# W_down of a decoder trunk's MLP turned round: token blocks stand in the array, 512 weight columns move, and the sample's 32 tokens go unsplit through quarters of it

## Chip, cores and metric

One core of one Trainium2 chip runs the whole step as one program. Times are device microseconds (us) of that core. Three runs of the kernel before gave 2141.54, 2145.24 and 2144.73 us, median 2144.73. One more execution was profiled; its span, from the first instruction to the last, is 2147.1 us.

## The reference, cut to what matters

One layer of a decoder trunk for 256 prompt tokens and 32 sample tokens (8 x 4), all in float32, width D = 2048. The first part (input projection, four token-mixing branches, their merge, w_out) is the same in both kernels. What the change touches is the second sub-layer:

```
h = rmsnorm(x1, n_mlp_pre)                 # (tokens, 2048)
a = relu(h @ w_up) ** 2                    # w_up (2048, 8192)
f = a @ w_down                             # w_down (8192, 2048)
y = x1 + rmsnorm(f, n_mlp_post)            # y_prompt (256, 2048), y_sample (32, 2048)
```

## The kernel before

Activations lie transposed: 128 channels on the partitions, the 288 tokens (256 prompt, then 32 sample) in the columns. A dense product of the program is made exact enough by a split: an operand W is W = H + L, where H has the short mantissa of float32r and L is the rest, also float32r. Each product W x is then three float32r products, H xh, H xl and L xh, added up in PSUM.

**Weights.** `plan` lists the weight chunks (512 KB each, 1024 columns of a raw buffer) in the order of use and the jobs that use them. `w_load` issues a chunk's transfer on SyncE's queue into one of `RAWN` = 4 raw buffers. A chunk has two halves of 128 x 512. For a half, ScalarE writes H (`w_high`, a CAST) and VectorE writes L (`w_low`, a TENSOR_TENSOR subtract) into one of `HN` = 5 pairs of buffers. `w_split`, called after each tile of a half, lets these run up to four halves ahead of TensorE; `w_low` issues the next loads.

**Products.** `dense` goes over the halves of a group. A half of w_up or w_down is 2 tiles of K (128 rows each) by 256 weight columns. For each of the two output tiles of 128 channels, and each of the 2 tiles of K, three products are made: 128 x 128 weights stand, 288 token columns move. That is 12 products per half. PSUM banks rotate over five: `dps` (three), `holda`, `holdb`.

**The MLP.** The 8192 hidden channels come in four fourths (`nf = 4`): up (16 tiles of hidden channels, `ev_up`: relu, square, split into `tH`, `tL`), then down with those 16 tiles as K, over 16 output tiles. `ev_down` adds a fourth's product to `self.f` (channels on partitions, 288 tokens). In the last fourth it also adds up squares for the norm (`square`) and multiplies by the gain, and `lane_ftok` turns the result by 128 x 128 transposes so that tokens lie on the partitions. `finish` sums the squares by small products, makes the reciprocal root (`rsqrt`), adds x1 and stores y. The program is written out whole ahead of time; a planner (`Pace`) estimates when operands are there and interleaves the side work ("lanes") with the dense products. It counts no times on the chip; order on each engine is fixed by what it emits.

Every instruction goes through one helper, so nearly all have line L234; rows are told apart by tiles: `rfix` holds the split weights, `rt` holds `tH` and `tL`, `ffix` the raw weights and constants, `barena` the second half's float32 buffers, `rot` the banks of the lanes.

Of the kernel before, what the change touches and what calls it, by code (L numbers as in the profile page):

```python
# [10 lines left out]
ALU = mybir.AluOpType  # L11
# [25 lines left out]
class Tiles:  # L37
    """Columns lo..hi of each of some buffers, indexed as [:, tile, ...]."""
# [8 lines left out]
class Arena:  # L47
    """Blocks of columns. One given back is used again when its last use is estimated over, or if there is no other."""
# [66 lines left out]
class Step:  # L115
    """A chain of instructions: when its results will be there, when it goes on."""
# [5 lines left out]
class Pace:  # L122
    """An estimate of each engine's program in microseconds, so that work is emitted when its operands will be there."""
# [55 lines left out]
    def cost(self, eng, name, out, ins):  # L179
# [5 lines left out]
        if eng == "pe":  # L185
            if name == "transpose":
                return n * 2 / 2400
            return n * (1 if ins[-1].dtype == F32R else 4 if out.shape[0] > 32 else 1) / 2400
# [9 lines left out]
class Flags:  # L198
    """What is there, from when on."""
# [13 lines left out]
class Paced:  # L213
    """An engine whose instructions are counted."""
# [34 lines left out]
class Kern:  # L249
# [70 lines left out]
    def post(self, f):  # L320
        """f, which reads the last bank, behind the present unit."""
# [19 lines left out]
    def rsqrt_steps(self, y, v, t):  # L341
        """y = v ** -0.5 on the vector engine: a seed from the exponent's bits and Newton steps."""
# [91 lines left out]
    def gains(self):  # L434
        """Loads of the norms' gains as rows, the first one's before."""
# [9 lines left out]
    def vectors(self):  # L445
        """Loads of the other per-channel vectors and of the conv and pool states."""
# [29 lines left out]
    def lane_prep(self):  # L476
        """Columns of the vectors and of the states, by transposes."""
# [51 lines left out]
    def w_init(self, chunks):  # L529
# [8 lines left out]
        self.wh = [self.R.get(512).ap for _ in range(self.HN)]  # L538
        self.wl = [self.R.get(512).ap for _ in range(self.HN)]
        self.nload = 0  # L540
        self.nsplit = 0
        self.low, self.rawat = [], [0.0] * self.RAWN
        self.w_load()

    def w_load(self):
# [5 lines left out]
        raw = self.raw[i % self.RAWN]  # L551
        dst = raw[:, 0:nk * nc_].rearrange("p (k n) -> p k n", k=nk)
        if pad:
            self.nc.gpsimd.memset(raw[:, 0:nk * nc_], 0.0)
            at = 0
            for s in src:
                n = s.shape[-1]
                self.rawat[i % self.RAWN] = self.timed(lambda: self.nc.sync.dma_start(dst[:, :, at:at + n], s.rearrange("(k p) n -> p k n", p=128)))
                at += n
        else:  # L560
            self.rawat[i % self.RAWN] = self.timed(lambda: self.nc.sync.dma_start(dst, src.rearrange("(k p) n -> p k n", p=128)))

    def w_high(self):
        """Half a chunk of the split W = H + L: H, with float32r's mantissa."""
        i, k, n, nc_ = self.halves[self.nsplit]
        raw = self.raw[i % self.RAWN][:, k * nc_:(k + n) * nc_]
        h = self.wh[self.nsplit % self.HN][:, 0:n * nc_]
        l = self.wl[self.nsplit % self.HN][:, 0:n * nc_]
# [12 lines left out]
    def w_split(self, last):  # L581
        """Splits ahead, up to the half last, as far as their operands will be there."""
# [4 lines left out]
        if n <= last and n < len(self.halves) and self.rawat[self.halves[n][0] % self.RAWN] <= now + self.SOON[1]:  # L587
            self.w_high()

    def w_need(self, s):  # L590
        """The split of the half s."""
# [38 lines left out]
    def timed(self, f):  # L630
        """When the results of f will be there."""
# [27 lines left out]
    def room(self, *sizes):  # L659
        """Waits until blocks of these sizes can be had and some is left."""  # L660
# [35 lines left out]
    def bank(self):  # L696
        """The next bank for a tile's products, after the evacuation that reads it."""
# [12 lines left out]
    def dense(self, ci, nch, mts, x, evac, raw=0):  # L710
        """Groups of output tiles: chunks ci..ci+nch-1 over K, the tiles mts (tile, column offset)."""
# [8 lines left out]
        for s in hs:  # L720
            _, _, nk, ncol = self.halves[s]
            self.w_need(s)
            wh = self.wh[s % self.HN][:, 0:nk * ncol].rearrange("p (k n) -> p k n", k=nk)
            wl = self.wl[s % self.HN][:, 0:nk * ncol].rearrange("p (k n) -> p k n", k=nk)
            for m, off in mts:
# [12 lines left out]
                self.w_split(s + self.HN - 1)  # L738
# [6 lines left out]
    XRAW = 7  # L745

    def x_load(self, c):
        """Half the channels of x by tokens."""
# [22 lines left out]
    def x_init(self):  # L771
# [3 lines left out]
        # the first tiles' H, L, and their sums, which lie where k and v come later  # L775
# [1880 lines left out]
```

## Time and profile before

| what | value |
|---|---|
| runs, median (lowest to highest) | 2144.73 us (2141.54 to 2145.24) |
| profiled execution, span | 2147.1 us, 2.4 us above the median |
| TensorE busy | 2104.4 us, 98% of the span |
| VectorE / ScalarE busy | 60% / 45% |
| mean granted clock of TensorE | 0.985 of 2.4 GHz |
| four stretches of w_down products | 1411.3, 1616.1, 1820.8 and 2025.6 us to 2132.1 us |

How to read it: in the rows below, PE is TensorE's products and PEld its weight loads, DVE is VectorE, ACT is ScalarE. A product's own duration (about 0.3 us for 288 columns) is longer than its share of the engine, because products overlap; what one costs is read from start to start.

### The profile page before, as it was taken

Reading aid. Unit: us, or ns where it says so; the run is one execution under the profiler, and the core shown is the slowest. Engines: PE = TensorE matmul, PEld = TensorE weight load, DVE = VectorE, ACT = ScalarE, POOL = GpSimd, SP = SyncE. Lnnn points to the kernel's source line nnn. Section 1 sums busy time; section 2 is a strip of 40 time slices with the busy share of each in tenths; the row PEclk is TensorE's granted clock in tenths of the full one; section 3 lists DMA queues with packets and bytes.
Section 4 is the critical chain, followed back from the end, with each engine's and each line's share of the span. In section 5 each row is a group of like instructions: output and inputs, shape, how many; then the busy total and the mean of one; then the engine's idle time right before and its main releaser. Section 6 shows DMA issues by size and latency. Waiting matters only on the chain.

```text
span 2147.1 us, 43279 instructions
## 1 busy us (share of the span) xinstructions
PE 2104.4 (98%) x16452; PEld 2011.0 (94%) x16452; DVE 1280.3 (60%) x2534; ACT 968.6 (45%) x1864; POOL 74.4 (3%) x324
## 2 busy tenths in 40 slices
PE   7999999999999999999999999999999999999997
PEld 6999999999877788899999998999999999999997
DVE  4769997778754555465555547544555455445554
ACT  4445543335433333344444555644444344334454
POOL 4101100101000000000000000000000000000000
PEclk7999999999999999999999998999999999999998
DMA  5697777867788777656555653555555555555553
GB/s 157 190 244 203 187 189 198 223 170 211 216 232 267 227 231 216 197 149 168 165 164 169 202 158 109 155 168 162 163 164 170 164 163 165 167 166 162 164 158 113
DMA packets 359956, 388.98 MB, mean 181 GB/s; under 512 B 20729, under 2 KB 334259, under 8 KB 355652
## 3 DMA queue, kind: packets, MB, share of 16 engines
q1 hardware_dynamic: 359748, 386.22, 62.2%
q8 instruction: 129, 2.11, 0.4%
q14 instruction: 79, 0.65, 0.1%
HBM read 374.94 MB, written 11.23 MB: 180 GB/s over the span
## 4 chain that ended last, share of the span: by engine, by line
PE 92%; DMA 3%; DVE 2%; SPq 1%; issue 1%; ACT 0%; DVEq 0%; ACTq 0%
PE dps L234 66%; PE holda L234 11%; PE holdb L234 8%; PE rot L234 7%; DVE arena L234 1%; DMA arena<-cache_sb_k 1%; DMA arena<-state_ssm_h 1%; SPq L234 1%; DVE rfix L234 1%; DMA arena<-state_dn_conv 1%; DMA ffix<-w_in 1%; DVE barena L234 0%; DMA arena<-state_dn_s 0%; SPq L1265 0%; DMA arena<-x_prompt 0%
## 5 line engine op out<-in xcount | busy, mean ns | idle before, releaser
L234 PE MATMUL dps<-rfix 128*128 128x288 f32 x8124 | 1174.8, 299 | 6.7 <-DVE arena L234 2.7
L234 PEld LDWEIGHTS dps<-rfix 128*128 128x128 f32 x8124 | 1105.3, 189 | 47.4 <-issue 26.7
L234 DVE TENSOR_TENSOR rfix<-ffix,rfix 128x512 fp32r<-128x512 f32 x1124 | 764.0, 688 | 571.1 <-ACT rfix L234 562.0
L234 ACT CAST rfix<-ffix 128x512 fp32r<-128x512 f32 (+1 forms) x1125 | 691.8, 620 | 848.9 <-PE dps L234 680.7
L234 PE MATMUL dps<-rt,rfix 128*128 128x288 f32 x1824 | 261.9, 295 | 0.0
L234 PEld LDWEIGHTS dps<-rt,rfix 128*128 128x128 f32 x1824 | 249.5, 188 | 0.0
L234 PE MATMUL dps<-ro,rfix 128*128 128x288 f32 x960 | 140.1, 298 | 0.0
L234 PEld LDWEIGHTS dps<-ro,rfix 128*128 128x128 f32 x960 | 130.4, 188 | 5.3 <-issue 3.7
L234 PE MATMUL rot<-arena 128*128 128x128 f32 (+7 forms) x804 | 103.8, 283 | 0.0
L234 PE MATMUL holda<-rfix 128*128 128x288 f32 x624 | 102.3, 297 | 0.0
L234 PE MATMUL holdb<-rfix 128*128 128x288 f32 x624 | 102.2, 297 | 0.0
L234 DVE STREAM_TRANSPOSE arena<-arena 128x512 f32<-128x512 f32 x136 | 95.2, 701 | 11.3 <-DMA arena<-cache_sb_k 11.1
L234 PEld LDWEIGHTS rot<-arena 128*128 128x128 f32 (+5 forms) x804 | 86.7, 182 | 14.5 <-issue 10.5
L234 PE MATMUL holdb<-rt,rfix 128*128 128x288 f32 x624 | 100.1, 295 | 0.0
L234 PE MATMUL holda<-rt,rfix 128*128 128x288 f32 x624 | 100.1, 295 | 0.0
L234 PEld LDWEIGHTS holdb<-rfix 128*128 128x128 f32 x624 | 89.9, 189 | 0.0
L234 PEld LDWEIGHTS holda<-rfix 128*128 128x128 f32 x624 | 89.9, 189 | 0.0
L234 PEld LDWEIGHTS holdb<-rt,rfix 128*128 128x128 f32 x624 | 88.8, 188 | 0.0
L234 PEld LDWEIGHTS holda<-rt,rfix 128*128 128x128 f32 x624 | 88.8, 188 | 0.0
L234 PE MATMUL rot<-ffix,arena 128*128 128x128 f32 (+11 forms) x416 | 65.5, 278 | 19.4 <-DMA arena<-state_ssm_h 6.3
L234 PEld LDWEIGHTS rot<-ffix,arena 128*128 128x128 f32 (+9 forms) x416 | 49.4, 148 | 26.3 <-issue 17.0
L234 PE MATMUL holda<-arena 128*32 128x128 f32 (+1 forms) x1280 | 68.7, 341 | 1.2 <-DVE arena L234 1.2
(121 smaller groups left out, 1064.0 us busy)
## 6 DMA issues: line engine op xcount, KB each, us to landing
ffix<-w_in SPq DMA_DIRECT2D x232, 512.0 KB
ffix<-w_up SPq DMA_DIRECT2D x128, 512.0 KB
ffix<-w_down SPq DMA_DIRECT2D x128, 512.0 KB
arena<-cache_sb_k SPq DMA_DIRECT2D x128, 256.0 KB
arena<-cache_sb_v SPq DMA_DIRECT2D x128, 256.0 KB
ffix<-w_branch SPq DMA_DIRECT2D x40, 512.0 KB
ffix<-w_out SPq DMA_DIRECT2D x32, 512.0 KB
arena<-state_dn_s SPq DMA_DIRECT2D x16, 256.0 KB
```

The lines of the kernel that those rows point to most:

```text
L234: return f(*args, **kw)
```

## The change

The job of w_down becomes `dense_tok`. Now a 128-token block of `tH` / `tL` stands and 512 columns of w_down move, so the output has tokens on the partitions. A half is one tile of K by 512 weight columns (chunks are 2 tiles of K by 512). Per half: for each of the two prompt blocks three products of 128 x 128 by 512. The 32 sample tokens are not in these. Every fourth half, four plain float32 products follow each other, one for each of the last four tiles of K: 32 sample tokens stand (from `ts32`, an unsplit copy written by GpSimd in `ev_up`), 512 raw weight columns move, and product q writes the PSUM rows 32q to 32q+31, so that it uses a quarter of the array's columns. The four quarters are sums over different tiles of K; they are added together at the end by a product with `e32` (four stacked identities). Raw chunks of w_down are kept until their sample products are made (`kept`); there are six raw buffers in the second half instead of four.

`ev_down` now evacuates three banks (two prompt blocks and the sample) of 128 x 512 per 512 output channels and fourth. The squares are summed along the row by ScalarE, the gain is a row vector loaded in advance on every partition, and `lane_ftok` is gone. `finish` squares and scales the sample's sum too.

```diff
     def w_low(self):
         _, i, *low = self.low.pop(0)
         self.tt(*low, ALU.subtract)
+        self.w_loads()
+
+    def w_loads(self):
         i = self.low[0][1] if self.low else self.halves[min(self.nsplit, len(self.halves) - 1)][0]
-        while self.nload < min(i + self.RAWN, len(self.chunks)):
+        i = min([i] + self.kept[0:1])
+        while self.nload < len(self.chunks) and self.rawholds[self.rawnext] < i:
             self.w_load()
...
+    def dense_tok(self, ci, nch, j, x, xs, evac):
+        ps = [self.bank() for _ in range(3)]
+        hs = [s for s in range(self.first[ci], len(self.halves)) if self.halves[s][0] < ci + nch]
+        for s in hs:
+            k = s - hs[0]
+            last = s == hs[-1]
+            self.used = s
+            self.w_need(s)
+            wh, wl = [w[:, 0] for w in self.w_half(s)]
+            th, tl = x(k)
+            if k % 4 == 3:
+                self.pump()
+                for q in range(4):
+                    c, i, _, n = self.halves[s - 3 + q]
+                    raw = self.raw[self.rawslot[c]][:, i * n:i * n + n]
+                    self.mm(ps[2][32 * q:32 * q + 32], xs(k - 3 + q), raw, k == 3, last)
+                self.kept = self.kept[2:]
+                self.w_loads()
...
+            for b in range(2):
+                self.pump()
+                c = slice(128 * b, 128 * b + 128)
+                self.mm(ps[b], th[:, c], wh, k == 0, False)
+                self.mm(ps[b], tl[:, c], wh, False, False)
+                self.mm(ps[b], th[:, c], wl, False, last)
+                self.flush()
+                self.w_split()
...
     def ev_up(self, m, ps):
...
+        self.nc.gpsimd.tensor_copy(self.ts32[:, m], w.ap[:, NP:NT])
...
     def ev_down(self, i, n):
         def f(m, ps):
-            fa = self.f[:, m]
+            j, b = m
+            fa = self.ft[b][:, 512 * j:512 * j + 512]
             if i == 0:
                 self.cp(fa, ps)
-                return
-            self.tt(fa, fa, ps, ALU.add)
+            else:
+                self.tt(fa, fa, ps, ALU.add)
...
-            self.square(m, fa)
-            self.cp(fa, fa, scale=self.gmpost[:, m:m + 1])
-            self.ready.add(("f", m))
+            yield
+            if b < 2:
+                t = self.B.get(512, hi=True)
+                self.act(t.ap, fa, AF.Square, accum_out=self.sq[:, 4 * b + j:4 * b + j + 1])
+                self.B.put(t)
+                self.tt(fa, fa, self.gb[:, 512 * j:512 * j + 512], ALU.mult)
+            else:
+                if j == 0:
+                    self.fsum = self.rot()
+                self.mm(self.fsum[32 * j:32 * j + 32], self.e32, fa)
         return f
...
     def finish(self):
-        for out, at, n in to:
-            for i, a in enumerate((self.acc1.ap, self.acc2.ap)):
-                self.mm(out, a[:, at:at + n], self.ones[:, 0:1], i == 0, i == 1)
+        fs, w = self.ft[2][:, 0:512], self.st2.ap[:, 48:49]
+        self.act(fs, self.fsum, AF.Square, accum_out=w)
+        self.tt(self.gs, self.fsum, self.gs, ALU.mult)
+        ps = self.rot()
+        self.mm(ps[:, 0:1], self.es, w)
+        nc.vector.tensor_reduce(out=v[:, 0:2], in_=self.sq.rearrange("p (b j) -> p b j", b=2), axis=AX.X, op=ALU.add)
+        nc.vector.tensor_copy(v[:, 2:3], ps[:, 0:1])
...
     def plan(self):
...
-            for m in range(0, KT, 2):
-                group(wdn, D * i, KT, 128 * m, 256, (m, m + 1), self.get_t, self.ev_down(i, nf))
-            if i == nf - 2:
-                call(lambda: self.lane(self.lane_ftok()))
+            for j in range(4):
+                first = len(chunks)
+                for k in range(0, KT, 2):
+                    self.kept.append(len(chunks))
+                    r = slice(D * i + 128 * k, D * i + 128 * k + 256)
+                    chunks.append((wdn[r, 512 * j:512 * j + 512], 2, 512, False))
+                jobs.append(("t", first, KT // 2, j, self.get_t, lambda k: self.ts32[:, k], self.ev_down(i, nf)))
```

On TensorE, at the start of the first w_down stretch, the kernel before has this (each row is a run of products of one output bank, the shape is that of the output; `rt` is the MLP's hidden activations, `rfix` the split weights):

```order
L234 MATMUL dps<-rfix 128x288 x102
L234 MATMUL holda<-rt,rfix 128x288 x6
L234 MATMUL holdb<-rt,rfix 128x288 x6
L234 MATMUL holda<-rt,rfix 128x288 x6
L234 MATMUL holdb<-rt,rfix 128x288 x6
```

The change has at the same place:

```order
L234 MATMUL dps<-rfix 128x288 x102
L234 MATMUL holda<-rfix,rt 128x512 x3
L234 MATMUL holdb<-rfix,rt 128x512 x3
L234 MATMUL holda<-rfix,rt 128x512 x3
L234 MATMUL holdb<-rfix,rt 128x512 x3
L234 MATMUL holda<-rfix,rt 128x512 x3
L234 MATMUL holdb<-rfix,rt 128x512 x3
L234 MATMUL dps<-ffix,barena 32x512 x4
L234 MATMUL holda<-rfix,rt 128x512 x3
L234 MATMUL holdb<-rfix,rt 128x512 x3
```

Twelve products of 288 columns per half became six of 512, and ahead of every fourth half's six stand the four products of the sample, with raw weights from `ffix` (or, for the two new buffers, from `barena`).

TensorE's end before, from the last dense products on (the small products sum the squares, the 128x128 and 32x128 ones are transposes):

```order
L234 MATMUL holdb<-rt,rfix 128x288 x6
L234 MATMUL rot<-ffix,barena 128x1 x4
L234 MATMUL rot<-ffix,barena 32x1 x8
L234 MATMUL rot<-ffix,barena 128x128 x8
L234 MATMUL rot<-ffix,barena 32x128 x4
```

and with the change:

```order
L234 MATMUL dps<-rfix,rt 128x512 x24
L234 MATMUL holda<-ffix,barena 32x512 x4
L234 MATMUL dps<-rfix,rt 128x512 x6
L234 MATMUL rot<-barena 32x512
L234 MATMUL rot<-barena 128x1
```

The transposes behind the last product are gone; one product that adds the sample's four quarters (`rot<-barena 32x512`) and one that spreads its sum of squares stand there instead.

VectorE's end with the change, from the additions of the last three banks to the first small step of the root (before, three additions of 128x288 and one square's sum stood ahead of that step):

```order
L234 TENSOR_TENSOR barena<-barena,holda 128x512
L234 TENSOR_TENSOR barena<-barena,dps 128x512 x2
L234 TENSOR_TENSOR barena<-barena 128x512 x2
L234 TENSOR_TENSOR barena<-rot,barena 128x512
L234 TENSOR_REDUCE barena<-barena 128x2
L234 COPY barena<-rot 128x1
L234 SCALAR_TENSOR_TENSOR barena<-barena 128x3
```

The gain's products (128x512 x2, and that from `rot`) now stand between the last additions and the root.

## Rows read from the trace of the kernel before

**Rows 1.** The page: busy time of the engines over the span, the granted clock by slices, and the chain that ended last.

```profile
PE 2104.4 (98%) x16452; PEld 2011.0 (94%) x16452; DVE 1280.3 (60%) x2534; ACT 968.6 (45%) x1864; POOL 74.4 (3%) x324
...
PEclk7999999999999999999999998999999999999998
...
GB/s 157 190 244 203 187 189 198 223 170 211 216 232 267 227 231 216 197 149 168 165 164 169 202 158 109 155 168 162 163 164 170 164 163 165 167 166 162 164 158 113
...
PE 92%; DMA 3%; DVE 2%; SPq 1%; issue 1%; ACT 0%; DVEq 0%; ACTq 0%
```

**Rows 2.** Busy time by stretch: the second and third w_down stretch, the fourth, and what follows it. Columns: stretch, its length, busy time and count of each engine, granted clock, DMA share, GB/s.

```profile
1616.00:1718.00 102.00, 102.00 (x767) 102.00 (x766) 49.72 (x82) 40.61 (x67) 0.00 (x0) 1.00 0.54 165
1821.00:1923.00 102.00, 102.00 (x768) 102.00 (x767) 49.72 (x82) 40.67 (x67) 0.00 (x0) 1.00 0.54 165
2025.60:2132.10 106.50, 106.50 (x806) 106.06 (x804) 53.34 (x92) 55.27 (x101) 0.00 (x0) 1.00 0.43 134
2132.10:2147.10 15.00, 3.33 (x37) 2.60 (x36) 8.44 (x20) 3.36 (x7) 0.00 (x0) 0.62 0.41 157
```

**Rows 3.** Order of time on TensorE inside the second w_down stretch: start, length of the run, products of one bank.

```profile
1700.06 0.96 PE L234 MATMUL holda<-rt,rfix 128*128 128x288 f32 x6
1700.86 0.96 PE L234 MATMUL dps<-rt,rfix 128*128 128x288 f32 x6
1701.66 0.96 PE L234 MATMUL holda<-rt,rfix 128*128 128x288 f32 x6
1702.46 0.96 PE L234 MATMUL dps<-rt,rfix 128*128 128x288 f32 x6
```

**Rows 4.** Order of time on TensorE in the sample's attention, where four float32 products in quarters of the array (`holda<-arena`, 32 columns stand, 512 move; each shows as two passes, so x8) stand between dense products of 288 columns.

```profile
851.68 1.07 PE L234 MATMUL holda<-arena 128*32 128x512 f32 x8
852.68 6.65 PE L234 MATMUL dps<-rfix 128*128 128x288 f32 x48
859.26 1.07 PE L234 MATMUL holda<-arena 128*32 128x512 f32 x8
860.26 6.65 PE L234 MATMUL dps<-rfix 128*128 128x288 f32 x48
866.84 1.07 PE L234 MATMUL holda<-arena 128*32 128x512 f32 x8
867.84 6.65 PE L234 MATMUL dps<-rfix 128*128 128x288 f32 x48
874.42 1.07 PE L234 MATMUL holda<-arena 128*32 128x512 f32 x8
```

**Rows 5.** Groups of TensorE instructions by shape: count, busy time, mean ns of one. The first two are float32 products on the whole array, two passes each, four products of each width; the last is w_down's own float32r product.

```profile
L234 PE MATMUL rot<-arena 128*128 128x512 f32 x8 | 4.1, 592 | 0.0
...
L234 PE MATMUL rot<-arena 128*128 128x288 f32 x8 | 2.6, 404 | 0.0
...
L234 PE MATMUL dps<-rt,rfix 128*128 128x288 f32 x1824 | 261.9, 295 | 0.0
```

**Rows 6.** Groups of VectorE and ScalarE instructions by shape, whole span: the split of a half, and work on 128 x 512 and 128 x 288 from PSUM or in place.

```profile
L234 DVE TENSOR_TENSOR rfix<-ffix,rfix 128x512 fp32r<-128x512 f32 x1124 | 764.0, 688 | 571.1 <-ACT rfix L234 562.0 <-PE holda L234 4.1 <-DMA arena<-cache_sb_v 1.4
...
L234 DVE TENSOR_TENSOR barena<-barena,dps 128x288 f32<-128x288 f32 x29 | 13.1, 451 | 16.6 <-PE dps L234 16.6
...
L234 DVE TENSOR_TENSOR arena<-arena,rot 128x512 f32<-128x512 f32 x16 | 11.0, 687 | 13.9 <-PE rot L234 13.8
...
L234 ACT CAST rfix<-ffix 128x512 fp32r<-128x512 f32 x1124 | 691.5, 620 | 848.9 <-PE dps L234 680.7 <-PE holda L234 65.3 <-PE holdb L234 59.9
...
L234 ACT ACTIVATE arena<-arena 128x512 f32<-128x512 f32 x14 | 8.5, 624 | 7.2 <-DVE arena L234 7.2
```

**Rows 7.** Groups inside the fourth w_down stretch: the transposes that `lane_ftok` put between its products.

```profile
L234 PE MATMUL rot<-ffix,barena 128*128 128x128 f32 x24 | 3.6, 272 | 0.0
...
L234 PE MATMUL rot<-ffix,barena 128*32 128x128 f32 x12 | 1.8, 271 | 0.0
```

**Rows 8.** Order of time at the end, all engines.

```profile
2130.37 0.96 PE L234 MATMUL holda<-rt,rfix 128*128 128x288 f32 x6
2131.04 0.85 PEld L234 LDWEIGHTS holdb<-rt,rfix 128*128 128x128 f32 x6
2131.17 0.96 PE L234 MATMUL holdb<-rt,rfix 128*128 128x288 f32 x6
...
2134.87 0.16 DVE L234 SCALAR_TENSOR_TENSOR barena<-rot,barena 128x3 f32<-128x3 f32 x1 [1.71 <-PE rot L234]
...
2136.84 6.06 DVE L234 SCALAR_TENSOR_TENSOR barena<-barena 128x3 f32<-128x3 f32 x8
2138.01 4.58 SPq L234 DMA_DIRECT2D out_y_prompt<-barena  x5
2142.93 1.84 SPq L234 DMA_DIRECT2D out_y_sample<-barena  x4
```

More of the change, by code (lines that the diff above doesn't have):

```diff
@@ L187, in cost @@
                 return n * 2 / 2400
-            return n * (1 if ins[-1].dtype == F32R else 4 if out.shape[0] > 32 else 1) / 2400
+            return n * (4 if ins[-1].dtype != F32R else 1) / (4 if out.shape[0] <= 32 else 1) / 2400
         if eng == "act":
@@ L537, in w_init @@
         self.raw = [self.A.get(self.CW).ap for _ in range(self.RAWN)]
-        self.wh = [self.R.get(512).ap for _ in range(self.HN)]
-        self.wl = [self.R.get(512).ap for _ in range(self.HN)]
+        self.rawholds, self.rawslot, self.rawnext = [-1] * self.RAWN, {}, 0
+        self.ring = [(self.R.get(512).ap, self.R.get(512).ap) for _ in range(self.HN)]
+        self.holds = [-1] * self.HN
+        self.at, self.used, self.slot = 0, 0, {}
         self.nload = 0
         self.nsplit = 0
-        self.low, self.rawat = [], [0.0] * self.RAWN
+        self.low, self.rawat = [], {}
         self.w_load()
@@ L550, in w_load @@
         src, nk, nc_, pad = self.chunks[i]
-        raw = self.raw[i % self.RAWN]
+        raw = self.raw[self.rawnext]
+        self.rawholds[self.rawnext], self.rawslot[i] = i, self.rawnext
+        self.rawnext = (self.rawnext + 1) % len(self.raw)
         dst = raw[:, 0:nk * nc_].rearrange("p (k n) -> p k n", k=nk)
@@ L576, in w_low, with w_free, w_more, w_half @@
         self.tt(*low, ALU.subtract)
+        self.w_loads()
+    def w_loads(self):
         i = self.low[0][1] if self.low else self.halves[min(self.nsplit, len(self.halves) - 1)][0]
-        while self.nload < min(i + self.RAWN, len(self.chunks)):
+        i = min([i] + self.kept[0:1])
+        while self.nload < len(self.chunks) and self.rawholds[self.rawnext] < i:
             self.w_load()
-    def w_split(self, last):
+    def w_free(self):
+        return self.holds[self.at] < self.used
+    def w_more(self, bufs):
+        self.raw += bufs
+        self.rawholds += [-1] * len(bufs)
+    def w_half(self, s):
+        _, _, nk, ncol = self.halves[s]
+        return [w[:, 0:nk * ncol].rearrange("p (k n) -> p k n", k=nk) for w in self.ring[self.slot[s]]]
+    def w_split(self):
         now = self.pace.t["pe"]
@@ L586, in w_split @@
         n = self.nsplit
-        if n <= last and n < len(self.halves) and self.rawat[self.halves[n][0] % self.RAWN] <= now + self.SOON[1]:
+        if n < len(self.halves) and self.w_free() and self.rawat[self.halves[n][0]] <= now + self.SOON[1]:
             self.w_high()
@@ L2310, in lane_x1tok, with gains @@
                 yield self.POST
-                self.cp(self.tok(0, b, slice(128 * k0, 128 * k0 + 512)), ps[0:n, :])
+                self.cp(self.tok(b, slice(128 * k0, 128 * k0 + 512)), ps[0:n, :])
                 yield
-        s = self.B.get(2048, hi=True)
-        e, es = self.B.get(32, hi=True), self.B.get(128, hi=True)
+        def gains():
+            g = self.I['norm_mlp_post']
+            nc.sync.dma_start(self.gb, g.broadcast_to([128, D]))
+            for q in range(4):
+                nc.sync.dma_start(self.gs[32 * q:32 * q + 32], g[:, 512 * q:512 * q + 512].broadcast_to([32, 512]))
+        self.later(gains)
+        s = Buf(self.xTb.ap[:, 0:D], None, 0)
+        e, es = self.B.get(32), self.B.get(128)
+        self.e32, self.es = e.ap, es.ap
         nc.vector.tensor_reduce(out=e.ap, in_=self.ident.rearrange("p (j c) -> p c j", j=4), axis=AX.X, op=ALU.add)
@@ L2353, in f @@
-            self.ready.add(("f", m))
-        return f
-    def lane_ftok(self):
-        for k0 in range(0, KT, 4):
-            while ("f", k0 + 3) not in self.ready:
-                yield
-            for b, (at, n) in enumerate(BLK):
-                ps = self.rot()
-                for k in range(4):
-                    self.tr(ps[0:n, 128 * k:128 * k + 128], self.f[:, k0 + k, at:at + n])
-                yield self.POST
-                self.cp(self.tok(1, b, slice(128 * k0, 128 * k0 + 512)), ps[0:n, :])
-                yield
-        self.ready.add("ftok")
+            yield
@@ L2372, in finish @@
[L2372 to L2377 removed]
+        while self.evacs:
+            self.pace.t["pe"] += 0.25
+            self.pump()
@@ L2542, in phase2 @@
         self.st2 = self.B.get(64)
+        self.ts32 = self.B.get(KT * NS).v("p (k n) -> p k n", k=KT)
+        self.w_more([self.B.get(self.CW).ap for _ in range(2)])
         self.lane(self.lane_xT())
```

56 lines of the change are left out of this document (35 added, 21 removed).

## The prediction

> **What bounds the kernel now.** The page first: TensorE is busy 98% of the span and the chain that ended last lies on it for 92% [rows 1]. Whatever the change does to TensorE's time it does to the total, unless another engine falls behind. Then the stretches: in the w_down stretches TensorE is busy all of the time at clock 1.00 (2.4 GHz), VectorE 49% and ScalarE 40% of it, DMA engines 0.54 at 165 GB/s [rows 2]. So these stretches cost exactly the products on TensorE, and everything else has about half its time free.
>
> What one product costs is seen in the order of time: runs of six start 0.80 us apart, so 133.3 ns from start to start for 288 columns [rows 3]. A stretch of a fourth is 16 output tiles x 16 tiles of K x 3 = 768 products, 102.4 us; four of them are **409.6 us**. The last stretch takes 106.5 us, 4.1 us more [rows 2]: 36 transposes stand in it [rows 7].
>
> 288 columns at 2.4 GHz are 120.0 ns, so 13.3 ns of each 133.3 are not streaming. That remainder decides this case, because the change makes half as many products.
>
> **The change, part by part.**
>
> *Prompt products.* Per tile of K and 512 output channels, 4 x 3 products of 288 columns become 2 x 3 of 512. There are 4 x 4 x 16 = 256 such units, so 3072 products become 1536. The trace of before has no float32r product of 512 columns. Streaming 512 columns is 213.3 ns. Lower bound: float32 products stream two cycles a column, and what a pass of theirs costs is its group's busy time per product less one duration: 4.1/4 - 0.592 = 0.433 us at 512 columns and 2.6/4 - 0.404 = 0.246 at 288 [rows 5], 0.835 ns a column with next to nothing left over; half of 0.433 is 216 ns for 512 columns at one cycle each. Upper bound: the 13.3 ns grow with the columns, 133.3 x 512/288 = 237.0 ns. Between them I take the 13.3 ns as a fixed cost of each product, **226.7 ns**: each product of either kernel has one load of 128 columns of weights in front of it, which runs beside the product before it (a run's six loads start 0.13 us ahead of its six products, [rows 8]), and that load does not grow with the moving columns. The nearest row is the float32r product of 288 columns, which has the remainder; the float32 passes, which have none, are another kind. 1536 x 0.2267 = 348.2 us.
>
> *Sample products.* Every fourth tile of K four float32 products of 512 columns go through quarters of the array: 64 groups. Exactly this form, four products with 32 standing and 512 moving columns between dense float32r products, stands in the sample's attention. Groups start 7.58 us apart with 48 dense products between them: 7.58 - 48 x 0.1333 = **1.18 us a group** [rows 4]. The eight passes run side by side (1.07 us for eight of about 0.6 us each), so the quarters do work at once; two passes alone would be 2 x 0.433 = 0.87 us [rows 5], and 0.31 us are lost where the array changes from whole to quarters and back. 64 x 1.18 = 75.5 us. Bounds: 0.87 and 1.18 (the row is of the same form, so I take it).
>
> Together 348.2 + 75.5 = 423.7 us against 409.6: **+14.1 us**. The column count alone would not say so: per unit 12 x 288 = 3456 columns become 6 x 512 = 3072, and the sample's 4 x 2 x 2 x 512 cycles in four quarters per four units are 512 a unit more.
>
> *End of the last fourth.* The 4.1 us of transposes leave the last stretch. Three products with `e32` enter it (the fourth is behind the last dense product). Each is one float32 product of 512 columns in a quarter: between 0.87 and 1.18 us, I take 1.18, since the array changes twice for each; +3.5. Net **-0.6 us**.
>
> *Behind the last product.* Before, the last run of products starts at 2131.17 and lasts 0.96, so ends at 2132.13; the first small step of the root starts 2.74 us later, and from there to the end of the span it is 12.2 us [rows 8]. With the change, T being the end of the last product: the first prompt block's products end about 0.68 us earlier, so VectorE's two additions of 128 x 512 (0.69 each, [rows 6]) end at about T + 0.8. ScalarE squares both blocks and then the sample's sum (0.62 each): done at about T + 2.1. VectorE's product of the sample with its gain waits for that, 0.69; with a short sum and a copy behind it (about 0.16 each, as the root's steps of three columns, [rows 8]) the root starts at about T + 3.3. From there the steps are the same as before. **+0.6 us**.
>
> *What costs nothing.* The split of a half is the same work as before, 0.69 us of VectorE and 0.62 of ScalarE [rows 6], under 6 x 0.227 = 1.36 us of TensorE instead of 1.60; evacuating three banks of 128 x 512 per 16 halves adds about 2.1 us of VectorE under 26.5 us. ScalarE and VectorE may run four halves ahead, 5.4 us; were that cover gone, TensorE would still wait for neither, since 0.69 is under 1.36. The 64 GpSimd copies of 128 x 32 lie beside up products, on an engine with no busy time in these stretches [rows 2]. The gain rows (about 1.3 MB on chip) load during the first up products behind six full raw buffers; at 165 GB/s that is 8 us against 6 chunks x 3.2 us.
>
> *Loads.* A pair of w_down chunks is given back only after its sample group, and the pair that goes there is needed nine halves and two groups later, 9 x 1.36 + 2 x 1.18 = 14.6 us, less 1.5 us for its split. A pair is 1.05 MB, 6.4 us at the 165 GB/s of these stretches [rows 2], and the page shows slices at up to 267 GB/s [rows 1]. On SyncE's queue only loads of the same kind stand behind a waiting one. If this cover were gone, every microsecond of lateness would count 64 times.
>
> Sum: -409.6 + 348.2 + 75.5 - 0.6 + 0.6 = **+14.1 us**. On the profiled execution, 2147.1 + 14.1 = 2161.2. That execution's span is 2.4 us above the median of the runs shown, so against the median 2144.7 + 14.1 = **2158.8, say 2159 us**, 0.66% slower.
>
> **A page against a row.** A product in a row costs 133.3 ns for 288 columns [rows 3], 13.3 above streaming. The Trainium skill, page "TensorE: Matmul & The Clock Gate", section "Wait — 56ns, not 53.3ns?", states for matmuls back to back at full clock that start to start is the columns over 2.4 GHz plus about 2.5 ns. For 288 that would be 122.5, which this trace does not show; for 512 it would be 215.8 ns, and the change would come to 1536 x 0.2158 + 75.5 - 409.6 = -2.6 us, no change that can be measured. What it would do here is the first rival.
>
> **The rivals.**
> 1. *The remainder hides behind the longer stream.* If the 13.3 ns are a weight load that is not quite ready after 120 ns, a stream of 213 ns covers it and a product costs 216 ns [rows 5]: 331.8 + 75.5 - 409.6 = -2.3, 2142.4 us, the same. For it: float32 passes with the same load show no remainder. Against: no row shows a load that is late by itself, and a load of the same 128 columns is not late in front of those passes.
> 2. *The remainder grows with the columns* (a limit on how fast a float32r stream is read): 237.0 ns, 364.0 + 75.5 - 409.6 = +29.9, 2174.6 us. For it: only float32r shows the remainder, and it streams twice as fast as float32. Against: nothing in the trace separates it from the fixed cost.
> 3. *The change of the array is hidden*, and a sample group costs its two passes, 0.87 us. With 226.7 ns: 348.2 + 55.7 - 409.6, and 0.9 less for the `e32` products: -6.6, 2138.1 us, **faster**. It decides from a group price of 0.90 us down. Against: three periods in a row give 1.18 [rows 4].
> 4. *Weights come late*: a pair of chunks lands after its time. With 0.3 us lost per group, +14.1 + 19 gives 2178. Against: 6.4 us needed, 13 there.
>
> **How the numbers follow.** Chances: forecast 0.60, rival 1 0.16, rival 2 0.13, rival 3 0.06, rival 4 0.05. The forecast's own range is 2153 to 2165 (a product between 223 and 230 ns, a ns being 1.5 us). The range takes in rivals 1 and 2 and leaves 3 and 4 out: **2141 to 2175**. About 0.2% (4.3 us) is what a measurement of this kernel can tell from no change. Slower by more: forecast, rivals 2 and 4, 0.76; same: rival 1 and a little of the forecast's edge, 0.17; faster: 0.07.
>
> **What would show it.** In the profile after, inside a w_down stretch: 24 products of 512 columns from group to group, 6.6 us apart in all; if the stretch is 105.9 us the two prices are right together, and a run of products alone tells 226.7 from 216 or 237. TensorE should have no idle time there; a wait for DMA at the sample products means rival 4. The end should take about 15.6 us behind the last dense product instead of 15.0. I am wrong above all if a product of 512 columns costs 216 ns, since then nothing is left of the loss.

## The result, and the profile after

Four runs of the changed kernel took 2162.88 to 2174.88 us, median **2169.03**; four of the kernel before, beside them, 2141.54 to 2146.89, median 2144.98. The ratio is 1.0129, interval 1.0102 to 1.0157: slower, as forecast, but by 24 us and not by 14. The execution profiled after has a span of 2173.1 us, 26.0 above the 2147.1 of the one before.

The page of after, busy time and the chain that ended last, answers to [rows 1]:

```profile
PE 2123.7 (98%) x15366; PEld 1885.0 (87%) x15366; DVE 1284.2 (59%) x2519; ACT 954.2 (44%) x1834; POOL 88.8 (4%) x388
...
PE 93%; DMA 3%; DVE 2%; SPq 1%; issue 0%; ACT 0%; DVEq 0%; ACTq 0%
```

TensorE has 1086 instructions fewer and is busy 19 us longer; the chain still lies on it. By stretch, after, the answer to [rows 2] (the four w_down stretches and what follows; columns: stretch, length, busy time and count of each engine, granted clock, DMA share, GB/s):

```profile
core 0: us, PE busy (x) PEld busy (x) DVE busy (x) ACT busy (x) POOL busy (x), PEclk, DMA share, GB/s
1412.70:1521.40 108.70, 108.70 (x515) 73.39 (x514) 45.72 (x68) 46.56 (x78) 0.42 (x2) 1.00 0.45 146
1623.80:1732.40 108.60, 108.60 (x514) 73.33 (x513) 51.36 (x79) 40.49 (x67) 0.42 (x2) 1.00 0.46 146
1834.80:1943.50 108.70, 108.70 (x515) 73.39 (x514) 51.45 (x79) 40.53 (x68) 0.42 (x2) 1.00 0.45 146
2045.90:2158.00 112.10, 112.10 (x521) 73.35 (x519) 52.64 (x81) 42.02 (x75) 0.42 (x2) 1.00 0.38 122
2158.00:2173.10 15.10, 1.41 (x5) 0.41 (x4) 10.50 (x25) 1.99 (x6) 0.00 (x0) 0.69 0.41 156
```

TensorE is busy for the whole of each stretch, at clock 1.00 (2.4 GHz), and the DMA share has fallen from 0.54 to 0.45: no transfer is waited for, the products themselves cost more. A stretch takes 108.66 us (from the start of its first product to the start of the first one behind it; the windows of the rows are rounded to 0.1) where 102.4 stood (105.9 forecast), the fourth, up to the end of its last dense product, 112.2 for 106.5. Three times 6.26, 5.7 and 0.1 of the end are 24.6 us; the other 1.4 to 1.5 lie ahead of the first stretch, which began at 1411.3 and now begins at 1412.7 behind the same products.

Inside the second stretch, in order of time on TensorE (start, length, what, how many; a float32 product shows as two passes, so x8 is a group of four), where [rows 3] and [rows 4] stood before:

```profile
1709.55 1.06 PE L234 MATMUL dps<-barena 128*32 128x512 f32 x8
1710.55 5.87 PE L234 MATMUL dps<-rfix,rt 128*128 128x512 f32 x24
1716.35 1.07 PE L234 MATMUL dps<-ffix,barena 128*32 128x512 f32 x8
1717.34 5.87 PE L234 MATMUL dps<-rfix,rt 128*128 128x512 f32 x24
1723.14 1.07 PE L234 MATMUL dps<-ffix,barena 128*32 128x512 f32 x8
```

From group to group are 6.80 and 6.79 us; the forecast was 24 x 0.2267 + 1.18 = 6.62. The 0.17 us more, 64 times, are 11 us; the end came out 0.5 us better than forecast, which leaves the 10.5 us that it missed. What the rows don't say is how the 0.17 us divide between products and groups.

### The profile page after: what moved, and what is told of

It reads as the page before. It is cut to its first block, busy times and chain, and to the rows that moved or that the text cites. A ratio compares the mean times of both kernels' runs of the same rounds, so it can differ in the third digit from the quotient of the medians.

```text
span 2173.1 us, 41304 instructions
## 1 busy us (share of the span) xinstructions
PE 2123.7 (98%) x15366; PEld 1885.0 (87%) x15366; DVE 1284.2 (59%) x2519; ACT 954.2 (44%) x1834; POOL 88.8 (4%) x388
## 4 chain that ended last, share of the span: by engine, by line
PE 93%; DMA 3%; DVE 2%; SPq 1%; issue 0%; ACT 0%; DVEq 0%; ACTq 0%
PE dps L234 67%; PE holda L234 11%; PE holdb L234 8%; PE rot L234 7%; DVE arena L234 1%; DMA arena<-state_ssm_h 1%; SPq L234 1%; DMA arena<-state_dn_conv 1%; DVE barena L234 1%; DMA ffix<-w_in 1%; DVE rfix L234 1%; DMA out_k_prompt<-arena 0%; DMA arena<-state_dn_s 0%; DMA arena<-cache_sb_v 0%; ACT arena L234 0%
## 5 line engine op out<-in xcount | busy, mean ns | idle before, releaser
L234 DVE TENSOR_TENSOR rfix<-ffix,rfix 128x512 fp32r<-128x512 f32 x936 | 635.6, 686 | 480.2 <-ACT rfix L234 472.1
L234 ACT CAST rfix<-ffix 128x512 fp32r<-128x512 f32 (+1 forms) x937 | 577.0, 620 | 760.3 <-PE dps L234 608.7
L234 PE MATMUL dps<-rfix,rt 128*128 128x512 f32 x912 | 239.6, 400 | 0.0
L234 PEld LDWEIGHTS dps<-rfix,rt 128*128 128x128 f32 x912 | 167.8, 188 | 72.6 <-ACT rfix L234 32.7
L234 DVE TENSOR_TENSOR rfix<-barena,rfix 128x512 fp32r<-128x512 f32 x188 | 128.8, 691 | 125.7 <-ACT rfix L234 122.4
L234 ACT CAST rfix<-barena 128x512 fp32r<-128x512 f32 x188 | 115.4, 619 | 141.2 <-PE dps L234 82.1
L234 DVE STREAM_TRANSPOSE arena<-arena 128x512 f32<-128x512 f32 x136 | 95.1, 701 | 12.2 <-DMA arena<-cache_sb_k 11.9
L234 PE MATMUL holda<-rfix,rt 128*128 128x512 f32 x336 | 97.8, 399 | 0.0
L234 PE MATMUL holdb<-rfix 128*128 128x288 f32 x576 | 94.1, 296 | 0.0
L234 PE MATMUL holdb<-rfix,rt 128*128 128x512 f32 x288 | 83.9, 399 | 0.0
L234 PEld LDWEIGHTS holda<-rfix,rt 128*128 128x128 f32 x336 | 62.0, 188 | 24.8 <-ACT rfix L234 10.9
```

The lines of the kernel that those rows point to most:

```text
L234: return f(*args, **kw)
```

## The experiments

Diffs are against the changed kernel, but for the last one. "Stretch" is the second w_down stretch unless another is named.

**The changed kernel again**, beside the experiments, with no edit:

> The changed kernel as it is, on the same chip as the next runs. Expected 2169 us, 1.013 of the kernel before; w_down stretches of 108.7 us, a 512-column product at 233.3 ns, a sample group at 1.19 us.

2164.26 us (2162.47 to 2168.94), ratio 1.0104, 1.0061 to 1.0147, against 2143.65. The stretch is 108.66 us again. What differs from the result above lies ahead of the first stretch, which begins at 1400.3 us in this profile and at 1412.7 in that one.

**Sample groups left out**, 48 of 64, so that long runs of prompt products stand alone:

```diff
-                for q in range(4):
+                for q in range(4 if last else 0):
...
-                    self.mm(ps[2][32 * q:32 * q + 32], xs(k - 3 + q), raw, k == 3, last)
+                    self.mm(ps[2][32 * q:32 * q + 32], xs(k - 3 + q), raw, True, True)
```

> Leaves out 48 of the 64 sample groups (of each 512 output channels only the last four tiles of K reach the sample). If a group costs 1.19 us, as its form did before, a stretch is 89.6 + 4 x 1.19 = 94.4 us and the time 57 us under the changed kernel's, about 2112 us, 33 us faster than before. If the change of the array were hidden and a group cost its two passes (0.87 us), 42 us under, about 2127. The prompt products stay at 233.3 ns either way.

2104.91 us, 59.4 less than the changed kernel beside it. The start of the stretch, on TensorE, and the stretch itself:

```profile
1603.52 20.92 PE L234 MATMUL dps<-rfix,rt 128*128 128x512 f32 x90
1624.37 1.06 PE L234 MATMUL holda<-barena 128*32 128x512 f32 x8
1625.36 1.67 PE L234 MATMUL dps<-rfix,rt 128*128 128x512 f32 x6
```

```profile
1603.50:1697.00 93.50, 93.50 (x418) 72.54 (x417) 51.41 (x79) 40.52 (x67) 0.42 (x2) 1.00 0.49 164
```

Ninety products before the group's start: 20.85 / 90 = 231.7 ns. The step into the group is longer than the others (0.33 us), and so are the first steps behind one; with these left out it is **230.9 ns** from start to start. 384 of them are 88.65 us, so the four groups left cost (93.52 - 88.65) / 4 = 1.22 us each, and the sixteen of the changed kernel (108.66 - 88.65) / 16 = **1.25 us** each. Both prices of the forecast were low: 4.2 ns a product and 0.07 us a group. The division is not quite sharp: in the changed kernel itself, products past the sixth of a run of 24 start 232.7 ns apart, so some 0.03 of the 1.25 us lie between the groups.

**Groups of eight**, half as many, with the four quarters used twice in each:

```diff
-            if k % 4 == 3:
+            if k % 8 == 7:
...
-                for q in range(4):
+                for q in range(8):
-                    c, i, _, n = self.halves[s - 3 + q]
+                    c, i, _, n = self.halves[s - 7 + q]
...
-                    self.mm(ps[2][32 * q:32 * q + 32], xs(k - 3 + q), raw, k == 3, last)
+                    o = 32 * (q % 4)
+                    self.mm(ps[2][o:o + 32], xs(k - 7 + q), raw, k == 7 and q < 4, last and q > 3)
-                self.kept = self.kept[2:]
+                self.kept = self.kept[4:]
```

> The same products, but the sample's come eight at a time (two to a quarter) every eighth tile of K. If 0.32 us of a group are the change of the array and back, 32 of these are saved: 10 us under the changed kernel, about 2159 us, a stretch of 106.0 us, a group of eight at 2.05 us. If the loss is within the products themselves, no change: 2169. If raw weights that are kept twice as long come late, TensorE waits for DMA and the time is above 2169.

2151.24 us, 13 less than the changed kernel; against before still 1.0038, 1.0017 to 1.0059. The stretch, and a piece of it on TensorE:

```profile
1603.70:1708.90 105.20, 105.20 (x514) 74.91 (x514) 50.47 (x79) 39.32 (x67) 0.42 (x2) 1.00 0.43 142
```

```profile
1613.44 1.06 PE L234 MATMUL holda<-barena 128*32 128x512 f32 x8
1614.32 1.04 PE L234 MATMUL holda<-ffix,barena 128*32 128x512 f32 x8
1615.30 11.37 PE L234 MATMUL dps<-rfix,rt 128*128 128x512 f32 x48
1626.60 1.06 PE L234 MATMUL holda<-ffix,barena 128*32 128x512 f32 x8
```

A group of eight costs (105.20 - 88.65) / 8 = 2.07 us. The second round adds 0.82 us by the stretches and 0.88 from start to start, about two passes of 0.433 [rows 5]. What is left of a group of four, some 0.4 us, is paid once per group whatever its length: (108.66 - 105.20) / 8 = 0.43 us for each group saved. So it goes with the change from whole products to quarters and back.

An obvious rival, that it is the change between float32r and float32, can be read in the kernel before. In its fourth stretch nine groups of four float32 transposes stand between the same dense products and add 3.94 us (from the first dense start to the last it is 106.21 us, 102.27 in the other stretches), 0.438 each, of which 4 x 0.108 = 0.432 are their own steps. Six groups have 128 columns standing, three have 32, like this one (PEld is the loads; the last counts end with the window):

```profile
2059.18 0.44 PEld L234 LDWEIGHTS rot<-ffix,barena 128*32 128x32 f32 x4
2059.31 0.60 PE L234 MATMUL rot<-ffix,barena 128*32 128x128 f32 x4
2059.64 0.43 PEld L234 LDWEIGHTS holdb<-rt,rfix 128*128 128x128 f32 x3
2059.66 0.51 PE L234 MATMUL holdb<-rt,rfix 128*128 128x288 f32 x2
```

So neither the type nor 32 standing columns by themselves cost the 0.4 us, as far as transposes stand for products. There the loads begin ahead of the products: at 2059.18 for 2059.31, and those of the next dense products before the transposes are through. At the sample group of the changed kernel that starts at 1716.35 (rows above) they do not:

```profile
1716.34 0.16 PEld L234 LDWEIGHTS dps<-ffix,barena 128*32 128x32 f32 x8 [0.37 <-issue]
1717.34 0.30 PEld L234 LDWEIGHTS dps<-rfix,rt 128*128 128x128 f32 x2 [0.84 <-ACT rfix L234]
```

The loads start together with their products, 1716.35 and 1717.34. Behind the group the second dense product starts 0.34 us after the first instead of 0.23. Loads that are not run ahead are thus a part of the 0.4 us; the rest is not divided further. The Trainium skill, page "TensorEngine Tiling (Array Packing)", section "Key Properties", says that changing the tiling mode drains TensorE, and gives no price. The 0.4 us and the late loads agree with that, but no run here shows that a drain is the cause.

**All products of a group in one quarter**:

```diff
-                    self.mm(ps[2][32 * q:32 * q + 32], xs(k - 3 + q), raw, k == 3, last)
+                    self.mm(ps[2][32 * q:32 * q + 32] if k == 3 else ps[2][0:32], xs(k - 3 + q), raw, k == 3, k == 3 and q > 0 or last and q == 3)
```

> In three of four groups all four sample products write the first quarter (the sums come out the same, since the quarters are added at the end). If the quarters work side by side, these groups now take 8 x 0.43 + 0.32 = 3.74 us instead of 1.19: 48 x 2.55 = +122 us, about 2291 us. If a group's price is not set by passes side by side, less than that.

2289.93 us (one execution), and the stretch:

```profile
1647.90:1786.80 138.90, 138.90 (x514) 81.16 (x513) 51.47 (x79) 40.48 (x67) 0.42 (x2) 1.00 0.37 117
```

(138.92 - 108.66) / 12 changed groups = 2.52 us more for each, 3.77 in place of 1.25. That is six passes of 0.42 more: in the changed kernel the four products do run side by side, and the quarters are not what went wrong.

So the question that is left is the 230.9 ns. Four experiments vary one thing in each fourth of w_down, on the kernel with few groups; each was executed once, so they are read from their stretches and not from their totals.

**Width of the moving operand**: 512, 384, 288 and 256 columns (the rest of the output is left out).

```diff
+    WIDTH = (512, 384, 288, 256)
...
+                w = self.WIDTH[fourth]
+                o = ps[b][:, 0:w]
-                self.mm(ps[b], th[:, c], wh, k == 0, False)
+                self.mm(o, th[:, c], wh[:, 0:w], k == 0, False)
...
```

> As e1_few_groups, and the prompt's products move 512, 384, 288 and 256 columns in the first to fourth fourth (the columns beyond are left out in the last three). Price of a product. A fixed remainder (the forecast's view, 13.3 ns): 226.7, 173.3, 133.3, 120.0 ns. A share of the columns (9.4%, from 233.3 at 512): 233.3, 175.0, 131.2, 116.7. Some of both (the line through 133.3 at 288 and 233.3 at 512: 0.446 ns a column and 4.8 ns): 233.3, 176.2, 133.3, 119.0. If turning round itself costs, 288 is not 133.3 here.

2000.09 us. On TensorE, the second stretch (384 columns) and the third (288):

```profile
1594.31 16.03 PE L234 MATMUL dps<-rfix,rt 128*128 128x384 f32 x90
1610.27 1.07 PE L234 MATMUL holda<-barena 128*32 128x512 f32 x8
...
1612.97 0.69 PE L234 MATMUL dps<-rfix,rt 128*128 128x384 f32 x3
1613.50 0.70 PE L234 MATMUL holdb<-rfix,rt 128*128 128x384 f32 x3
...
1769.70 0.56 PE L234 MATMUL dps<-rfix,rt 128*128 128x288 f32 x3
1770.11 0.56 PE L234 MATMUL holdb<-rfix,rt 128*128 128x288 f32 x3
1770.50 0.56 PE L234 MATMUL dps<-rfix,rt 128*128 128x288 f32 x3
```

15.96 / 90 = 177 ns at 384 columns; 0.80 / 6 = 133 ns at 288, the very price of [rows 3], although there weights stood and tokens moved. At 256 it is 119 (below, from the last experiment, where no supply limits it). With 230.9 at 512 the four lie within 2 ns of one line: (230.9 - 118.9) / 256 = **0.4375 ns a column, and about 7 ns a product**. Streaming at 2.4 GHz would be 0.4167. So of the 13.3 ns at 288 columns about half is fixed and half grows: neither the forecast (all fixed) nor rival 2 (all growing) but the middle of the two.

**Width of the standing operand**: 128, 96, 64 and 32 columns, 512 moving (the other output rows are left out).

```diff
+    STAND = (128, 96, 64, 32)
...
+                n = self.STAND[fourth]
+                c = slice(128 * b, 128 * b + n)
+                o = ps[b][0:n]
-                self.mm(ps[b], th[:, c], wh, k == 0, False)
+                self.mm(o, th[:, c], wh, k == 0, False)
...
```

> As e1_few_groups, and of each block of 128 tokens 128, 96, 64 and 32 stand in the first to fourth fourth (the others are left out), 512 columns move. If the 20 ns above streaming belong to the weight load beside the product, they shrink with the columns loaded: 233.3, 228, 223, 218 ns. If they belong to the moving stream, all four are 233.3 ns.

2108.29 us. The stretches with 96 and with 64:

```profile
1603.80:1697.10 93.30, 93.30 (x417) 62.24 (x416) 51.27 (x79) 40.54 (x68) 0.42 (x2) 1.00 0.49 164
1799.50:1892.50 93.00, 93.00 (x418) 51.94 (x417) 51.29 (x78) 40.51 (x68) 0.42 (x2) 1.00 0.49 165
```

The weight loads' busy time falls from 72.5 to 62.2 and 51.9 us while the stretch hardly moves (93.5, 93.3, 93.0), and within runs a product costs 231 ns at every width, 32 too. The size of the load in front of a product is not what makes it 17.6 ns longer than its 213.3 ns of streaming, and that load was the reason on which the forecast took the remainder as fixed. Every product in these runs still has a load of its own, so a fixed price per load is not excluded. Only behind a sample group does the size show: from the first dense product to the second it is 319, 297, 274 and 254 ns with 128, 96, 64 and 32 columns standing (means over each stretch's groups of the start-to-start times).

**Banks, adding, and what is read**: in the second stretch the two blocks' products alternate between banks, in the third each product overwrites instead of adding, in the fourth the moving operand is every second column, 256 of 512.

```diff
...
+                if fourth == 2:
+                    self.mm(ps[b], th[:, c], wh, True, True)
...
+                elif fourth == 3:
+                    vh, vl = [w.rearrange("p (n two) -> p two n", two=2)[:, 0] for w in (wh, wl)]
+                    self.mm(o, th[:, c], vh, k == 0, False)
...
```

> As e1_few_groups. First fourth unchanged; second: the two blocks' products take turns, so that no two in a row add to the same bank; third: each product overwrites its bank instead of adding (the sums are left out); fourth: 256 moving columns that lie two apart (half of the columns are left out). If the remainder is the adding in PSUM, the second or third falls from 233.3 towards 216 ns; if it is the moving stream's reading, both stay at 233.3. If the moving stream is read in pieces of two neighbouring columns, the fourth costs as much as 512 columns, about 230 ns; if each column is read for itself, as 256 columns, 117 to 120 ns.

2113.14 us. The second and third stretch, then the start of the fourth on TensorE:

```profile
1608.70:1702.20 93.50, 93.50 (x418) 72.55 (x417) 51.42 (x78) 40.78 (x68) 0.42 (x2) 1.00 0.49 164
1804.60:1898.10 93.50, 93.50 (x418) 72.56 (x417) 51.39 (x79) 40.52 (x67) 0.42 (x2) 1.00 0.49 164
```

```profile
2001.20 0.87 PE L234 MATMUL holda<-rfix,rt 128*128 128x256 f32 x3
2001.88 0.87 PE L234 MATMUL dps<-rfix,rt 128*128 128x256 f32 x3
2002.57 0.86 PE L234 MATMUL holda<-rfix,rt 128*128 128x256 f32 x3
```

93.5 us both times, as with few groups alone: neither the order of banks nor the adding in PSUM costs anything here. But 256 columns that lie two apart cost 0.685 / 3 = 228 ns, nearly the price of 512 beside each other and not the 119 of 256. At this stride the price is that of the 512 columns of memory spanned and not of the 256 multiplied; no other stride was run.

**Products alone**: in the second stretch no transfers and no splits, and one fixed moving operand; in the third the fixed operand alone.

```diff
+    def dense_alone(self, j, evac):
...
+        w = self.xh[:, 0:2].rearrange("p k n -> p (k n)")[:, 0:512]
...
+                self.mm(ps[b], th[:, c], w, k == 0, False)
+                self.mm(ps[b], tl[:, c], w, False, False)
+                self.mm(ps[b], th[:, c], w, False, k == KT - 1)
...
```

> As e1_few_groups; in the second fourth w_down is neither loaded nor split, and the 384 prompt products run on one fixed operand in the split activations' buffer, with VectorE, ScalarE and the transfers nearly idle; in the third fourth loads and splits go on as usual, but the moving operand is that fixed one. If the 15 ns that a 512-column product costs above its stream (231 against 213) come from other engines and transfers at the same memory, the second fourth falls towards 214 to 218 ns; if only from the splits writing next to the columns being read, the third does too. If it is how the stream is read, all four fourths stay at 231 ns.

2099.26 us. The second stretch:

```profile
1598.60:1687.00 88.40, 88.40 (x386) 72.16 (x385) 6.13 (x11) 1.69 (x4) 0.42 (x2) 1.00 0.02 6
```

With VectorE busy 6 us instead of 51, ScalarE 2 instead of 41 and the DMA engines at 0.02, its 384 products take 88.52 us, 230.5 ns each; the third stretch takes 93.52 as before. Other engines and transfers are not the cause.

**Groups of eight, and the sample's sum at one place** (the four `e32` products follow each other, instead of one per 512 output channels):

```diff
...
-                if j == 0:
+                if j == 3:
                     self.fsum = self.rot()
-                self.mm(self.fsum[32 * j:32 * j + 32], self.e32, fa)
+                    for q in range(4):
+                        self.mm(self.fsum[32 * q:32 * q + 32], self.e32, self.ft[2][:, 512 * q:512 * q + 512])
```

> As e5_groups8, and the four products that add the sample's quarters stand together behind the last dense product, each in a quarter of its own, instead of one per 512 output channels. If each of the three inside the stretch costs a change of the array and two passes (1.2 us) and the four together cost what one did, 3.5 us under e5_groups8: about 2148 us, 1.002 of the kernel before. If they cost more at the end than they save, as e5_groups8: 1.004.

From the start of its first dense product to that of its last, the fourth stretch falls from 108.41 us with groups of eight alone to 104.97, 3.4 less. The medians show only 0.8 of it: 2150.46 us, ratio 1.0032, 1.0014 to 1.0049, against 2144.01. Totals of one kernel spread by 10 us and more, so 3 us between two medians can't be told here. With groups of eight alone (1.0038) it is the best that was run with W_down turned, and it is still slower than the kernel before. By the prices above, groups of sixteen would make a stretch 88.65 + 4 x (2.07 + 2 x 0.82) = 103.5 us, an estimate that still lies above 102.4. But four times that 1.1 us is little more than the 3.9 us of transposes that the last stretch of before has besides, so with the sum at one place such a kernel would come out about even with the one before; it wasn't run.

**The kernel before with the sample left out** of w_down in the second to fourth fourth (diff against the kernel before):

```diff
...
+                    out, xh, xl = out[:, 0:width], xh[:, 0:width], xl[:, 0:width]
                     self.mm(out, a, xh, k0 + k in (0, raw), False)
...
```

> The kernel before, with the sample's 32 columns left out of w_down's products in the second to fourth fourth (256 columns move instead of 288). By the prices of the widths run (133.3 ns at 288, 119.3 at 256) a stretch falls from 102.4 to 91.6 us, 32 us in all, about 2112 us: then the sample cost 43 us in all four fourths before, against about 79 us in 64 groups now. If products of 256 columns are held up (by loads or weights), a stretch falls less.

2107.06 us, ratio 0.9839, 0.9811 to 0.9867. The first stretch (288 columns) and the second (256):

```profile
1401.70:1504.10 102.40, 102.40 (x770) 102.40 (x769) 45.77 (x68) 45.90 (x82) 0.00 (x0) 1.00 0.53 165
1606.50:1697.80 91.30, 91.30 (x770) 91.30 (x769) 49.47 (x83) 40.67 (x67) 0.00 (x0) 1.00 0.58 184
```

768 products in 91.3 us are 118.9 ns each. So before, the prompt alone would cost 3072 x 0.1189 = 365.2 us, and the sample as 32 more columns 409.6 - 365.2 = 44.4. Now the prompt costs 1536 x 0.2309 = 354.7 and the sample 64 x 1.25 = 80.0. **Turning the prompt's products saves 10.6 us; taking the sample out of the stream costs 35.6.** Together +25. Of the 35.6 us, 64 x 0.43 = 27.5 are the changes of the array; without them a group's two passes, 0.82 us by the groups of eight, would make 52.5 against the 44.4 of before.

## Why the prediction was right in its sign and short in its size

The 2169.03 us lie in the range of 2141 to 2175, but above the forecast's own 2153 to 2165. The range reaches so far only because it takes in rival 2, which had a chance of 0.13.

*The bound* held: TensorE is busy all of the four stretches after, as before, so the change is worth what its products cost.

*Prompt products: the step that failed.* The forecast took the 13.3 ns above streaming at 288 columns as a fixed cost of each product, because a load of 128 columns stands in front of each. 226.7 ns were forecast, 230.9 measured: 1536 x 4.2 = 6.5 us of the miss. The size of the load isn't the cause (231 ns with 128 or 32 standing columns), and the price grows by 0.4375 ns a column with some 7 ns fixed. Rival 2 had half of it right. Rival 1 (the remainder hides behind the longer stream, 216 ns) is refuted by every run of products. The Trainium skill, page "TensorE: Matmul & The Clock Gate", section "Wait — 56ns, not 53.3ns?", would give 215.8 ns for 512 columns, an estimate by its formula; the traces give 230.9, and the measurement decides.

*Sample products: right in kind, a little low.* 1.18 us from the groups of the attention, 1.25 measured: 64 x 0.07 = 4.5 us. Two passes and a change of the array were the right parts, 0.85 and 0.40. Rival 3 (the change hidden, 0.87) is refuted by the groups of eight, where 0.43 us are saved for each group dropped. Why a group in the attention costs 0.07 less is open, but for the 0.03 that lie in the dense products between the groups.

*The count of columns* would have given the sign after all, other than the prediction says: by its own numbers 3072 + 512 = 3584 columns stand against 3456, 128 more a unit, and 256 units of 128 columns at 2.4 GHz are 13.7 us, close to its +14.1.

*End of the last fourth: right.* From the first dense start to the last, the last stretch takes 111.79 us after and the others 108.44: 3.35 us for the three `e32` products (3.5 forecast), in the place of 106.21 - 102.27 = 3.94 us of transposes. The prediction has 4.1 for these, because it set the end of the last product against the start of the next; its net of -0.6 us came out.

*Behind the last product: 0.5 too much.* The order of time at the end of after, answer to [rows 8] (rows of one engine between these are left out):

```profile
2156.38 1.67 PE L234 MATMUL dps<-rfix,rt 128*128 128x512 f32 x6
...
2157.39 1.38 DVE L234 TENSOR_TENSOR barena<-barena,dps 128x512 f32<-128x512 f32 x2 [0.19 <-PE dps L234]
...
2159.44 0.58 ACT L234 ACTIVATE barena<-rot 128x512 f32<-128x512 f32 x1
...
2160.17 0.68 DVE L234 TENSOR_TENSOR barena<-rot,barena 128x512 f32<-128x512 f32 x1
2160.77 0.15 DVE L234 TENSOR_REDUCE barena<-barena 128x2 f32<-128x8 f32 x1
2160.84 0.15 DVE L234 COPY barena<-rot 128x1 f32<-128x1 f32 x1
2161.02 0.16 DVE L234 SCALAR_TENSOR_TENSOR barena<-barena 128x3 f32<-128x3 f32 x1
```

The last product ends at 2158.05. VectorE's additions end at +0.7 (forecast +0.8), ScalarE's squares at about +2.0 (+2.1), and the root begins at +2.97 (+3.3), because the short sum starts under the end of the product with the gain. From there to the end it is 12.1 us for 12.2 before. The end takes 15.1 us in all, 0.1 more than before, where 0.6 more were forecast.

*What was to cost nothing* cost nothing: no transfer is waited for at the sample's products, the splits keep ahead. Rival 4 is out.

The sum with the measured prices: 14.1 + 6.5 + 4.5 - 0.5 = 24.6 us, against 24.6 in the profiles outside the start and 24.1 between the medians.

*What stays open* is why a column costs 0.4375 ns and a product 7 ns on top. Shown is only what it is not: the number of standing columns, bank order, adding in PSUM, the other engines, transfers. A fixed price of the load that each product has in front of it was not tried. For the 0.4 us of a sample group it is shown that they are paid once per group and that the loads there start late; that a drain of the array is behind it is argued.

## What to carry to other kernels

A price measured at one width says nothing of how it splits into a part per instruction and a part per column; when a change trades many narrow products for few wide ones, look for a second width in the trace or keep both splits in the sum. Columns that ride along in a stream which must run anyway cost about their share of it (32 of 288 columns, 44 of 410 us); here the same tokens beside it cost 80 us, although four products run side by side there. Small products in quarters of the array should be gathered into long groups, since in this kernel each change of the array costs about 0.4 us however many follow.

## What the runs showed that had not been expected

- A moving operand of every second column cost as much as the memory that it spans: 256 columns two apart cost 228 ns, 256 adjacent ones 119.
- A product's price did not depend on which operand was weights and which tokens, nor, within a run, on how many columns stand (128 to 32): 133 ns at 288 columns in both kernels, 231 at 512.
- The stretches repeat between executions to about 0.01 us, while the start of the first one varied from 1396.1 to 1412.8 us among kernels with the same products ahead of it. The mean granted clock of these executions goes with it, from 0.994 at 1396.1 to 0.984 at 1412.8, while it is 1.00 in the stretches shown. The spread of the totals comes from there, so a change inside the stretches is read more sharply from them than from the totals.
